# Output projection over heads 0, 1, 2 and 4 as filler of the fourth head's attention and recurrence

## The chip, the cores and the metric

The kernel runs on one core of one Trainium2 chip. The metric is the time of one execution on the device, in microseconds (us). TensorE is called PE in the profile's rows, VectorE DVE, ScalarE ACT, GpSimd POOL; SP is the engine whose queue issues nearly all DMAs.

## The reference, cut to what matters

One encoder layer over 1024 tokens of width 1024, all in float32. Four attention heads and four recurrent heads work side by side on the normalised input; their eight outputs of 128 columns are put next to each other and go through one output projection:

```
h = rmsnorm(x); proj = h @ w_in
o_da = diff_attention(...)       # 4 heads: softmax map 0 - lam * softmax map 1, times v; rmsnorm
o_hg = hgrn2_bidirectional(...)  # 4 heads: gated linear recurrence, both directions; rmsnorm * silu(g)
x = x + concatenate([o_da, o_hg]) @ w_out
x = x + conv_glu(rmsnorm(x), ...)
x = x + (p @ w_ple) * sigmoid(rmsnorm(x) @ w_ple_gate)
out = rmsnorm(x)
```

The change is about the last attention and recurrent heads and the line with `w_out`.

## The kernel before, in words

Every large matrix product is made of three float32r products (high by high, high by low, low by high part), which `mm3` (L151) issues; `split_into` (L143) makes the two parts, the high one on ScalarE, the low one on VectorE or GpSimd.

The program is written as generators. `attn(h)` (L631) yields after each step: a step is the scores of one tile of 128 queries against 1024 keys, with both softmax maps at once in the two buffers B of PSUM (L656), negated maxima on VectorE (L662), exponentials on ScalarE (L664) and their combination on VectorE (L670); or the transposes and value matmuls of the tile before (L682, L686). `hgrn(h)` (L465) yields after each of seven levels (L486 to L509): eight matmuls into a buffer B, updates of K, Y and F on VectorE and GpSimd, and a masked copy of B into A on VectorE (L508). It then yields "v", and goes on with K transposed, the states, the 22 output matmuls (L542 to L546, two matrix passes each), the norm and the transposed output `oT[4 + h]`. The outputs of heads 0, 1, 2, 4, 5, 6 (`SPILLED`, L29; numbers from 4 on are the recurrent heads) are stored to DRAM (`od`, L730), and `head` (L736) loads them again and splits them.

`filler` (L1374) is one stream of the other products: the input projections of the heads, in order, and at the end the first half of the output projection, `out_a`. The stream carries marks ("hq3": head 3's q and gates are done; "hv3": its v and g). `fill(mark)` draws from the stream until the mark comes, or until it is empty; `fill(None, t)` draws until pieces of t us, by the numbers in the yields, are taken, and passes over marks. The loop at the end of `build` (L1423) puts them together for each head: 13 or 14 steps of attention, `fill("hq")`, then the recurrent head, each of its steps followed by one step of attention, and at "v" the rest of the attention and `fill("hv")`.

The order in which these are written is not the order in which they run. When the program is built (`schedule_with_timeline_sim=True`), a planner with its own durations picks, for each engine, among the instructions that are ready and have their buffers, those written first; what is written later moves up where an engine would be idle. `load` (L163) ties a DMA issue to stand behind the last store but one (`lag`) on SP's queue. On the chip each engine runs its list in that fixed order.

`out_a` (L755) multiplies the four attention heads (four `osp` tiles with both parts) by the first 512 rows of `w_out`, 16 pieces (`out_piece`, L748) of 128 tokens by 512 columns, and adds each piece to the rows of x that `load_x` has put into eight buffers of the pool `c` (15 buffers). `out_b` (L790) multiplies the four recurrent heads by the other 512 rows, adds, stores the sum to `xd` in DRAM, and goes on with the norm, the transposes and the first units of the gated MLP.

Of the kernel before, what the change touches and what calls it, by code (L numbers as in the profile page):

```python
# [16 lines left out]
P = 128  # L17
# [5 lines left out]
TAIL = "tail"  # L23
# [3 lines left out]
MAGIC = 12582912.0  # L27

SPILLED = (0, 1, 2, 4, 5, 6)  # L29

_PI_DIGITS = "3.14159265358979323846264338327950288419716939937510582097494459230781640628620899"

# [38 lines left out]
class Net:  # L71
# [155 lines left out]

    def setup(self):
        nc, t, g = self.nc, self.t, self.g
        cst = g.tile([P, 136], F32, name="cst")  # L230
        nc.scalar.dma_start(out=cst, in_=t["cst"])
        self.ident = cst[:, 0:128]
        self.invf = cst[:, 128:136]
        self.gb = self.gb_load("norm_mix_g")

        z = self.small(P, "warm", bufs=1)
        nc.gpsimd.memset(z, 0.0)
        ps = self.Sm()
        for _ in range(18):
            nc.tensor.matmul(ps[:, 0:128], z, z, start=True, stop=True)  # L240

    def setup2(self):
        nc, t, g = self.nc, self.t, self.g
        self.msk = g.tile([P, 8, P], U8, name="msk")
        mf = self.c([8, P])
        nc.sync.dma_start(out=mf, in_=t["msk"])
        nc.gpsimd.tensor_copy(self.msk, mf)
        st = self.c([P])
        nc.gpsimd.memset(st, 0.0)
        nc.sync.dma_start(out=st[0:66, :], in_=t["ffn_conv_w"].rearrange("o j (f p) -> (o j f) p", p=P))  # L250
        nc.sync.dma_start(out=st[66:88, :], in_=t["ffn_conv_b"].rearrange("o (f p) -> (o f) p", p=P))
        nc.sync.dma_start(out=st[88:104, :], in_=t["hg_lb_gamma"].rearrange("z l (h p) -> (z l h) p", p=P))
        nc.sync.dma_start(out=st[104:105, :], in_=t["da_subln_g"])
        nc.sync.dma_start(out=st[105:106, :], in_=t["hg_norm_g"])
        ps = self.Sm()
        nc.tensor.transpose(ps[:, 0:128], st, self.ident)
        cols = self.cols = g.tile([P, P], F32, name="cols")
        nc.vector.tensor_copy(cols, ps[:, 0:128])
        self.cw = lambda j, f: cols[:, j * 22 + f: j * 22 + f + 1]
        self.cb = lambda f: cols[:, 66 + f: 67 + f]  # L260
        self.norm_g = cols[:, 105:106]
        self.subln = g.tile([P, 1], F32, name="subln")
        nc.vector.tensor_scalar(self.subln, cols[:, 104:105], 1.0 - LAMBDA_INIT, None, ALU.mult)

        gam = cols[:, 88:104].rearrange("p (z l h) -> p z l h", z=2, l=2)
        mx = self.small(8, "lbm").rearrange("p (z h) -> p z h", z=2)
        e0 = self.small(8, "lb0").rearrange("p (z h) -> p z h", z=2)
        e1 = self.small(8, "lb1").rearrange("p (z h) -> p z h", z=2)
        nc.vector.tensor_tensor(out=mx, in0=gam[:, :, 0, :], in1=gam[:, :, 1, :], op=ALU.max)
        nc.vector.tensor_tensor(out=e0, in0=gam[:, :, 0, :], in1=mx, op=ALU.subtract)  # L270
        nc.vector.tensor_tensor(out=e1, in0=gam[:, :, 1, :], in1=mx, op=ALU.subtract)
        nc.scalar.activation(e0, e0, AF.Exp)
        nc.scalar.activation(e1, e1, AF.Exp)
        nc.vector.tensor_tensor(out=e1, in0=e0, in1=e1, op=ALU.add)
        nc.vector.reciprocal(e1, e1)
        self.lb = g.tile([P, 2, 4], F32, name="lb")
        self.lb1 = g.tile([P, 2, 4], F32, name="lb1")
        nc.vector.tensor_tensor(out=self.lb, in0=e0, in1=e1, op=ALU.mult)
        nc.vector.tensor_scalar(self.lb1, self.lb, -1.0, 1.0, ALU.mult, ALU.add)

        lam = self.c([4, 64])
        for i, nm in enumerate(("lam_q1", "lam_k1", "lam_q2", "lam_k2")):
            nc.sync.dma_start(out=lam[:, i, :], in_=t[nm].to_broadcast([P, 64]))
        nc.vector.tensor_tensor(out=lam[:, 0, :], in0=lam[:, 0, :], in1=lam[:, 1, :], op=ALU.mult)
        nc.vector.tensor_tensor(out=lam[:, 2, :], in0=lam[:, 2, :], in1=lam[:, 3, :], op=ALU.mult)
        ls = self.small(2, "lam")
        nc.vector.tensor_reduce(ls, vw(lam, [[128, 2], [1, 64]]), AX.X, ALU.add)
        nc.scalar.activation(ls, ls, AF.Exp)
        self.nlam = g.tile([P, 1], F32, name="nlam")
        nc.vector.tensor_tensor(out=self.nlam, in0=ls[:, 1:2], in1=ls[:, 0:1], op=ALU.subtract)  # L290
        nc.vector.tensor_scalar(self.nlam, self.nlam, -LAMBDA_INIT, None, ALU.add)

    def setup_rotary(self):
# [47 lines left out]
        for shift, nm in ((0.25, "cos16"), (0.0, "sin16")):  # L341
            v.tensor_scalar(r, acc, shift, None, ALU.add)
            rnd(q, r)
            v.tensor_tensor(out=r, in0=r, in1=q, op=ALU.subtract)
            v.tensor_scalar(r, r, 6.283185307179586, 3.1415925, ALU.mult, ALU.min)
            v.tensor_scalar(r, r, -3.1415925, None, ALU.max)
            tab = g.tile([P, 8, 2, 8], F32, name=nm)
# [376 lines left out]
        self.spill(h)  # L724


    def wout(self, r0, n, mk=None, lo_eng=None):
        return self.wrows(self.t["w_out"][0], r0, n * 512, 4, mk, lo_eng)

    def spill(self, i):  # L730

# [13 lines left out]
            else:  # L745
                self.split_into(hi, lo, self.oT[i][:, sl.start + o:sl.start + o + 512])

    def out_piece(self, s, n, wp, sp):  # L748
        ps = self.D()
        sl = slice(s * 128, s * 128 + 128)  # L750
        self.mm3(ps, [((sp[k][0][:, sl], sp[k][1][:, sl]), wp[k]) for k in range(4)])
        xs = self.xr[s][:, n * 512:n * 512 + 512]
        self.nc.vector.tensor_tensor(out=xs, in0=ps, in1=xs, op=ALU.add)

    def out_a(self):  # L755

        wp = self.wout(0, 0)
        yield
        sp = []
        for k in range(4):  # L760
            if k == 3:
                yield "heads"
            t = self.d([2, 1024], F32R, name="osp")
            self.head(t, k, slice(0, 1024))
            sp.append((t[:, 0, :], t[:, 1, :]))
        self.load_x()
        yield "x"
        for n in range(2):
            for s in range(NS):
                self.out_piece(s, n, wp, sp)  # L770
                yield 2.6
            if n == 0:
                wp = self.wout(0, 1)

# [15 lines left out]
    def out_b(self):  # L790

        nc = self.nc
        gb = self.gb_load("norm_ffn_g", self.wf([1024]))
        wps = [self.wout(512, 0, lo_eng=nc.vector),
               self.wout(512, 1, lambda: self.w2([2, 512]))]
        sp = None
        self.T = {}
        wg, wu = self.t["w_ffn_gate"][0], self.t["w_ffn_up"][0]
# [3 lines left out]
        for s in range(NS):  # L802
            if s % 4 == 0:
                sl = slice(s * 128, s * 128 + 512)
                sp = []
                for k in range(4):
                    o = self.c([2, 512], F32R, "osp")
                    self.head(o, 4 + k, sl)
                    sp.append(o)
            for n in range(2):  # L810
                ps = self.D()
# [98 lines left out]
        self.t_put("t4", t4, o, p)  # L910

    def load_x(self):
        nc, t = self.nc, self.t
        self.xr = []
        for i in range(8):
            xt = self.c([1024], name="x")
            self.load(out=xt, in_=t["x"][0, i * 128:(i + 1) * 128, :])
            self.xr.append(xt)

    def gb_load(self, name, gb=None):  # L920
# [407 lines left out]
    def build(self):  # L1328
# [4 lines left out]
        with tc.tile_pool(name="xa", bufs=8) as px:  # L1333
# [80 lines left out]
            def fill(mark=None, t=1e9):  # L1414

                while t > 0:
                    c = next(f, mark)
                    if c == mark:
                        return
                    if isinstance(c, float):  # L1420
                        t -= c

            for h in range(4):  # L1423
                at = self.attn(h, qk[h], v[h])
                for _ in range((13, 14, 14, 14)[h]):
                    next(at)
                fill("hq%d" % h)
                hg = self.hgrn(h, st[h])
                for c in hg:
# [4 lines left out]
                    if c is TAIL and h == 3:  # L1434
                        fill("x")
                if h < 3:
                    fill("da%d" % (h + 1))
                    fill(None, (15.6, 10, 10)[h])
                else:
                    fill()  # L1440
# [37 lines left out]
```

## Time and profile before

| | us |
|---|---|
| median of 3 runs | 1577.94 (1577.73 to 1578.14) |
| profiled execution | 1578.55 |
| its span | 1576.7 |
| TensorE busy | 1509.4 (96%) |
| VectorE busy | 1085.8 (69%) |
| GpSimd busy | 699.5 (44%) |
| ScalarE busy | 646.1 (41%) |

The span is the time from the first to the last instruction of the profiled execution; about 1.85 us of that execution lie around it. Busy times are of one execution. The granted clock is given as a share of TensorE's full speed, where the chip has two levels, 1.2 and 2.4 GHz; a value between is a mix of both in the stretch. A value in brackets behind a row of the timeline is the time that the engine was idle before, and the instruction whose end let it go on.

### The profile page before, as it was taken

How to read it: one execution, taken by the hardware profiler on the slowest of the kernel's cores; microseconds unless marked ns; L12 is line 12 of the kernel's file. 1: busy time of each engine (PE TensorE's matmuls, PEld its weight loads, DVE VectorE, ACT ScalarE, POOL GpSimd, SP SyncE). 2: the span in 40 equal slices, each digit the busy share in tenths (PEclk: the TensorE clock that was granted, in tenths of full speed). 3: DMA queues.
4: the chain of work that ended last, by engine and by line, in shares of the span. 5: the costliest groups of instructions: out<-in, count | busy, mean ns of one | idle time of the engine just before them, and what ended most of it. 6: DMA issues, size and time to landing. Idle time of an engine off the chain costs nothing. (4 is left out here: it accounts for less than half of the span.)

```text
span 1576.7 us, 21836 instructions
## 1 busy us (share of the span) xinstructions
PE 1509.4 (96%) x8550; PEld 1298.0 (82%) x8550; DVE 1085.8 (69%) x1617; ACT 646.1 (41%) x1082; POOL 699.5 (44%) x438
## 2 busy tenths in 40 slices
PE   8999999999999997999999999999999899899997
PEld 8969998999799885888778888888887677687886
DVE  7355576555655666757877766666658999986665
ACT  5335525642456255514543333333334233343222
POOL 3111541243105410520577666666657888785000
PEclk9999999999999998999999999999999899999999
DMA  8100011001100111213512222232227632131111
GB/s 247 41 14 15 28 54 41 28 28 41 41 15 28 54 54 40 104 58 130 165 29 93 91 83 87 85 95 82 90 85 251 203 107 80 31 120 47 34 51 40
DMA packets 92201, 118.59 MB, mean 75 GB/s; under 512 B 5200, under 2 KB 65858, under 8 KB 92098
## 3 DMA queue, kind: packets, MB, share of 16 engines
q1 hardware_dynamic: 91666, 116.34, 22.6%
q8 instruction: 67, 1.10, 0.3%
q10 hardware_dynamic: 432, 0.86, 0.2%
q14 instruction: 36, 0.29, 0.1%
HBM read 92.01 MB, written 23.07 MB: 73 GB/s over the span
## 5 line engine op out<-in xcount | busy, mean ns | idle before, releaser
L156 PE MATMUL D<-w,hT 128*128 128x256 f32 x1920 | 256.8, 289 | 0.7 <-POOL w L149 0.3
L156 PEld LDWEIGHTS D<-w,hT 128*128 128x128 f32 x1920 | 239.1, 193 | 3.1 <-issue 1.4
L149 POOL TENSOR_TENSOR w<-raw,w 128x1024 fp32r<-128x1024 f32 x41 | 101.8, 2486 | 277.8 <-ACT w L146 225.0
L156 PE MATMUL E<-T,S 128*128 128x512 f32 x924 | 217.1, 394 | 4.3 <-DVE ag L996 1.7
L149 POOL TENSOR_TENSOR S<-w,S 128x512 fp32r<-128x512 f32 x119 | 171.9, 1459 | 91.8 <-ACT S L146 71.6
L156 PEld LDWEIGHTS E<-T,S 128*128 128x128 f32 x924 | 175.3, 190 | 43.1 <-DVE ag L996 2.1
L156 PE MATMUL D<-hT,w 128*128 128x512 f32 x576 | 138.6, 396 | 0.0
L156 PEld LDWEIGHTS D<-hT,w 128*128 128x128 f32 x576 | 107.2, 189 | 24.7 <-issue 3.2
L156 PE MATMUL S<-T,S 128*128 128x512 f32 x528 | 124.2, 389 | 1.0 <-DVE T L149 1.0
L146 ACT ACTIVATE S<-w 128x512 fp32r<-128x512 f32 x121 | 73.3, 624 | 119.0 <-PE S L156 49.3
L156 PE MATMUL E<-op,op 128*128 128x512 f32 x432 | 107.5, 401 | 10.2 <-DVE x L1118 6.6
L156 PEld LDWEIGHTS S<-T,S 128*128 128x128 f32 x528 | 99.1, 188 | 22.0 <-DVE T L149 1.4
L156 PEld LDWEIGHTS E<-op,op 128*128 128x128 f32 x432 | 82.9, 194 | 31.6 <-DVE x L1118 8.3
L662 DVE TENSOR_REDUCE atm<-B 128x1 f32<-128x1024 f32 x64 | 75.3, 1218 | 44.2 <-PE B L656 44.2
L156 PE MATMUL D<-T,S 128*128 128x512 f32 x396 | 95.1, 391 | 4.1 <-ACT S L146 2.5
L149 POOL TENSOR_TENSOR S<-raw,S 128x512 fp32r<-128x512 f32 x30 | 47.4, 1580 | 99.1 <-ACT S L146 99.1
L156 PE MATMUL D<-w,osp 128*128 128x512 f32 x384 | 90.7, 392 | 0.0
L156 PEld LDWEIGHTS D<-T,S 128*128 128x128 f32 x396 | 73.9, 188 | 20.1 <-ACT S L146 2.7
L664 ACT ACTIVATE e<-B,atm 128x1024 f32<-128x1024 f32 x64 | 70.7, 1112 | 36.4 <-DVE atm L662 36.4
L156 PEld LDWEIGHTS D<-w,osp 128*128 128x128 f32 x384 | 71.2, 188 | 14.4
L156 PE MATMUL B<-wg,h 128*128 128x512 f32 x336 | 80.1, 393 | 0.0
L146 ACT ACTIVATE w<-raw 128x1024 fp32r<-128x1024 f32 x44 | 46.6, 1060 | 79.7 <-PE D L156 62.4
(288 smaller groups left out, 2937.0 us busy)
## 6 DMA issues: line engine op xcount, KB each, us to landing
md<-ag SPq DMA_DIRECT2D x22, 512.0 KB, 2.7
raw<-in_w_in SPq DMA_DIRECT2D x40, 256.0 KB, 3.2
raw<-in_w_ffn_gate SPq DMA_DIRECT2D x20, 512.0 KB, 3.9
w<-in_w_ffn_up SPq DMA_DIRECT2D x20, 512.0 KB, 3.9
mb<-md SPq DMA_DIRECT2D x40, 256.0 KB, 4.7
x<-in_x SPq DMA_DIRECT2D x16, 512.0 KB, 6.8
raw<-in_w_in SPq DMA_DIRECT2D x12, 512.0 KB, 4.0
raw<-in_w_ffn_down SPq DMA_DIRECT2D x12, 512.0 KB, 4.7
```

What stands on the lines that cost most here:

```text
L146: nc.scalar.activation(hi, src, AF.Copy)
L149: (lo_eng or nc.vector).tensor_tensor(out=lo, in0=src, in1=f32(hi), op=ALU.subtract)
L156: m = self.nc.tensor.matmul(out, a, b, start=new and i == 0 and j == 0, stop=i == n - 1 and j == 2, skip_group_check=not new)
L662: nc.vector.tensor_reduce(nm[:, m:m + 1], sc, AX.X, ALU.max, negate=True)
L664: self.last_exp = nc.scalar.activation(em, sc, AF.Exp, bias=nm[:, m:m + 1], accum_out=(s0 if m == 0 else s1)).ins
```

## The change

The first half of the output projection takes heads 0, 1, 2 and 4 (three attention heads and the first recurrent one), the second half heads 3, 5, 6 and 7. `wout` takes a list of heads and loads the weights of each by itself. `out_a` no longer keeps x on the chip: each piece loads its part of x into a buffer of the pool `raw` (3 buffers), adds, and stores the sum to `xd`; `load_x` loads `xd` when all pieces are done. For head 3, attention no longer runs ahead: after "hq3" each step of the recurrent head is followed by two steps of attention, and each but the one at "v" by 4.5 us of filler. The small constants, which had a tile each, become parts of one tile of 800 columns.

```diff
+FIRST, LAST = (0, 1, 2, 4), (3, 5, 6, 7)
...
+        G = g.tile([P, 800], F32, name="cst")
+        cst, self.g_cols, self.g_msk = G[:, 0:136], G[:, 136:264], G[:, 264:520]
+        self.g_rot = [G[:, 520 + 128 * i:648 + 128 * i] for i in range(2)]
...
-    def wout(self, r0, n, mk=None, lo_eng=None):
-        return self.wrows(self.t["w_out"][0], r0, n * 512, 4, mk, lo_eng)
+    def wout(self, heads, n, mk=None, lo_eng=None):
+        w, out = self.t["w_out"][0], []
+        for q in range(0, len(heads), 2):
+            mk = mk or (lambda: self.w([2, 512]))
+            hi, lo = mk(), mk()
+            raw = self.raw([2, 512])
+            for k in range(2):
+                r0 = heads[q + k] * P
+                self.load(out=raw[:, k, :], in_=w[r0:r0 + P, n * 512:n * 512 + 512])
+            self.split_into(hi, lo, raw, lo_eng or self.nc.gpsimd)
+            out += [(hi[:, k, :], lo[:, k, :]) for k in range(2)]
+        return out
...
     def out_a(self):
-        wp = self.wout(0, 0)
+        x = self.t["x"][0]
+        wp = self.wout(FIRST, 0)
         yield
         sp = []
-        for k in range(4):
-            if k == 3:
-                yield "heads"
+        for i in FIRST:
             t = self.d([2, 1024], F32R, name="osp")
-            self.head(t, k, slice(0, 1024))
+            self.head(t, i, slice(0, 1024))
             sp.append((t[:, 0, :], t[:, 1, :]))
-        self.load_x()
-        yield "x"
         for n in range(2):
+            cs = slice(n * 512, n * 512 + 512)
             for s in range(NS):
-                self.out_piece(s, n, wp, sp)
+                ps = self.D()
+                rs, sl = slice(s * P, (s + 1) * P), slice(s * 128, s * 128 + 128)
+                xs = self.raw([512])
+                self.load(out=xs, in_=x[rs, cs])
+                self.mm3(ps, [((sp[k][0][:, sl], sp[k][1][:, sl]), wp[k]) for k in range(4)])
+                self.nc.vector.tensor_tensor(out=xs, in0=ps, in1=xs, op=ALU.add)
+                self.store(out=self.xd[s][:, cs], in_=xs)
                 yield 2.6
             if n == 0:
-                wp = self.wout(0, 1)
+                wp = self.wout(FIRST, 1)
...
-        wps = [self.wout(512, 0, lo_eng=nc.vector),
-               self.wout(512, 1, lambda: self.w2([2, 512]))]
+        wps = [self.wout(LAST, 0, lo_eng=nc.vector),
+               self.wout(LAST, 1, lambda: self.w2([2, 512]))]
...
-                    self.head(o, 4 + k, sl)
+                    self.head(o, LAST[k], sl)
...
-            self.load(out=xt, in_=t["x"][0, i * 128:(i + 1) * 128, :])
+            self.load(out=xt, in_=self.xd[i])
...
-            for h in range(4):
+            for h in range(3):
                 at = self.attn(h, qk[h], v[h])
-                for _ in range((13, 14, 14, 14)[h]):
+                for _ in range((13, 14, 14)[h]):
                     next(at)
                 fill("hq%d" % h)
...
+            fill("hq3")
+            at = self.attn(3, qk[3], v[3])
+            for c in self.hgrn(3, st[3]):
+                next(at, None)
+                next(at, None)
+                if c == "v":
+                    self.run(at)
+                    fill("hv3")
+                elif isinstance(c, float):
+                    fill(None, 4.5)
+            fill()
+            self.load_x()
```

## Rows read from the trace of the kernel before

**Rows 1.** The page's slices: TensorE's busy tenths, and its granted clock.

```profile
PE   8999999999999997999999999999999899899997
PEclk9999999999999998999999999999999899999999
```

**Rows 2.** Windows: stretch, its length, then busy time of each engine, clock, DMA.

```profile
440.00:480.00 40.00, 40.00 (x331) 36.66 (x329) 22.29 (x38) 24.36 (x54) 5.97 (x3) 1.00 0.05 15
...
587.00:641.00 54.00, 40.63 (x280) 34.51 (x281) 34.72 (x56) 31.22 (x74) 7.15 (x5) 0.91 0.15 49
641.00:680.00 39.00, 36.21 (x265) 33.59 (x264) 32.72 (x42) 15.93 (x29) 23.04 (x23) 1.00 0.26 95
...
575.00:723.00 148.00, 130.69 (x866) 115.19 (x865) 97.06 (x163) 66.44 (x126) 37.39 (x30) 0.97 0.20 70
...
590.00:600.00 10.00, 7.47 (x39) 5.97 (x38) 6.37 (x10) 4.63 (x11) 0.00 (x0) 0.67 0.32 105
```

**Rows 3.** Waits of TensorE, 575 to 723: total, times, longest.

```profile
PE B L656 <- ACT e L664: 11.8, 6, 2.6
```

**Rows 4.** Timeline of TensorE, 555 to 740: start, duration, instruction.

```profile
581.30 4.55 PE L156 MATMUL D<-w,hT 128*128 128x256 f32 x36
...
589.48 3.45 PE L686 MATMUL S<-v,wT 128*128 128x128 f32 x16
...
610.95 1.65 PE L656 MATMUL B<-qkT,qkT 64*128 64x512 f32 x12 [2.17 <-ACT e L664]
...
613.02 2.01 PE L686 MATMUL S<-v,wT 128*128 128x128 f32 x16
...
617.64 1.65 PE L656 MATMUL B<-qkT,qkT 64*128 64x512 f32 x12 [2.17 <-ACT e L664]
...
642.28 2.88 PE L156 MATMUL D<-w,hT 128*128 128x256 f32 x22
...
648.72 4.08 PE L156 MATMUL D<-w,hT 128*128 128x256 f32 x32
652.64 1.95 PE L494 MATMUL B<-Y,X 128*128 128x128 f32 x16
...
714.21 22.04 PE L156 MATMUL D<-w,osp 128*128 128x512 f32 x96
```

**Rows 5.** Timeline of ScalarE, the g/v projection's first copy of head 3.

```profile
640.09 0.39 ACT L457 ACTIVATE v<-D 128x256 f32<-128x256 f32 x1
```

**Rows 6.** Timelines of VectorE and of GpSimd near 661.

```profile
661.34 2.89 DVE L504 TENSOR_TENSOR Y<-Y,F 128x512 f32<-128x512 f32 x1
664.15 1.32 DVE L508 COPY_PREDICATED A<-msk,B 128x1024 f32<-128x1024 uint8 x1
...
661.12 2.55 POOL L149 TENSOR_TENSOR w<-raw,w 128x1024 fp32r<-128x1024 f32 x1 [2.76 <-ACT w L146]
```

**Rows 7.** Timelines of TensorE, VectorE and ScalarE at recurrent head 3's end.

```profile
696.66 0.38 PE L546 MATMUL B<-St,Y 128*128 128x128 f32 x2
...
701.12 0.39 PE L544 MATMUL B<-St,Y 128*128 128x128 f32 x2
...
703.50 0.69 DVE L557 TENSOR_TENSOR o<-B,gs 128x512 f32<-128x512 f32 x1 [7.54 <-ACT sq L556]
...
711.97 0.69 DVE L563 TENSOR_TENSOR o<-o,hgy 128x512 f32<-128x512 f32 x1
...
714.06 0.69 ACT L570 ACTIVATE oT<-S,cols 128x512 f32<-128x512 f32 x1 [8.28 <-PE S L569]
```

**Rows 8.** DMA issues: count, size of each, median us to landing.

```profile
raw<-in_w_in SPq DMA_DIRECT2D x40, 256.0 KB, 3.2
...
x<-xd SPq DMA_DIRECT2D x8, 512.0 KB, 5.3
```

**Rows 9.** Timelines of SP's queue and of ScalarE.

```profile
667.44 0.42 SPq L167 DMA_DIRECT2D x<-in_x  x1
...
661.51 1.06 ACT L146 ACTIVATE w<-raw 128x1024 fp32r<-128x1024 f32 x1 [0.46 <-PE D L156]
```

More of the change, by code (lines that the diff above doesn't have):

```diff
@@ L229, in setup @@
         nc, t, g = self.nc, self.t, self.g
-        cst = g.tile([P, 136], F32, name="cst")
+        G = g.tile([P, 800], F32, name="cst")
+        cst, self.g_cols, self.g_msk = G[:, 0:136], G[:, 136:264], G[:, 264:520]
+        self.g_rot = [G[:, 520 + 128 * i:648 + 128 * i] for i in range(2)]
+        self.g_lb = [G[:, 776 + 8 * i:784 + 8 * i] for i in range(2)]
+        self.subln, self.nlam = G[:, 792:793], G[:, 793:794]
         nc.scalar.dma_start(out=cst, in_=t["cst"])
@@ L243, in setup2 @@
         nc, t, g = self.nc, self.t, self.g
-        self.msk = g.tile([P, 8, P], U8, name="msk")
+        self.msk = self.g_msk.bitcast(U8).rearrange("p (l t) -> p l t", l=8)
         mf = self.c([8, P])
@@ L256, in setup2 @@
         nc.tensor.transpose(ps[:, 0:128], st, self.ident)
-        cols = self.cols = g.tile([P, P], F32, name="cols")
+        cols = self.cols = self.g_cols
         nc.vector.tensor_copy(cols, ps[:, 0:128])
@@ L261, in setup2 @@
         self.norm_g = cols[:, 105:106]
-        self.subln = g.tile([P, 1], F32, name="subln")
         nc.vector.tensor_scalar(self.subln, cols[:, 104:105], 1.0 - LAMBDA_INIT, None, ALU.mult)
@@ L275, in setup2 @@
         nc.vector.reciprocal(e1, e1)
-        self.lb = g.tile([P, 2, 4], F32, name="lb")
-        self.lb1 = g.tile([P, 2, 4], F32, name="lb1")
+        self.lb, self.lb1 = [a.rearrange("p (z h) -> p z h", z=2) for a in self.g_lb]
         nc.vector.tensor_tensor(out=self.lb, in0=e0, in1=e1, op=ALU.mult)
@@ L288, in setup2 @@
         nc.scalar.activation(ls, ls, AF.Exp)
-        self.nlam = g.tile([P, 1], F32, name="nlam")
         nc.vector.tensor_tensor(out=self.nlam, in0=ls[:, 1:2], in1=ls[:, 0:1], op=ALU.subtract)
@@ L346, in setup_rotary @@
             v.tensor_scalar(r, r, -3.1415925, None, ALU.max)
-            tab = g.tile([P, 8, 2, 8], F32, name=nm)
+            tab = self.g_rot[len(self.rot)].rearrange("p (t j f) -> p t j f", t=8, j=2)
             rv = r.rearrange("p (t f) -> p t f", t=8)
@@ L746, in head @@
                 self.split_into(hi, lo, self.oT[i][:, sl.start + o:sl.start + o + 512])
[L748 to L753, printed above, removed]
     def out_a(self):
-        wp = self.wout(0, 0)
+        x = self.t["x"][0]
+        wp = self.wout(FIRST, 0)
         yield
         sp = []
-        for k in range(4):
-            if k == 3:
-                yield "heads"
+        for i in FIRST:
             t = self.d([2, 1024], F32R, name="osp")
-            self.head(t, k, slice(0, 1024))
+            self.head(t, i, slice(0, 1024))
             sp.append((t[:, 0, :], t[:, 1, :]))
-        self.load_x()
-        yield "x"
         for n in range(2):
+            cs = slice(n * 512, n * 512 + 512)
             for s in range(NS):
-                self.out_piece(s, n, wp, sp)
+                ps = self.D()
[5 more added lines that the diff above has]
+                self.store(out=self.xd[s][:, cs], in_=xs)
                 yield 2.6
             if n == 0:
-                wp = self.wout(0, 1)
+                wp = self.wout(FIRST, 1)
     def w2(self, shape, dt=F32R):
@@ L912, in load_x @@
     def load_x(self):
-        nc, t = self.nc, self.t
         self.xr = []
@@ L1421, in fill @@
                         t -= c
-            for h in range(4):
+            for h in range(3):
                 at = self.attn(h, qk[h], v[h])
-                for _ in range((13, 14, 14, 14)[h]):
+                for _ in range((13, 14, 14)[h]):
                     next(at)
                 fill("hq%d" % h)
-                hg = self.hgrn(h, st[h])
-                for c in hg:
+                for c in self.hgrn(h, st[h]):
                     next(at, None)
@@ L1433, in build @@
                         fill("hv%d" % h)
[L1434 to L1440, printed above, removed]
+                fill("da%d" % (h + 1))
+                fill(None, (15.6, 10, 10)[h])
+            fill("hq3")
[10 more added lines that the diff above has]
+            self.load_x()
         with tc.tile_pool(name="xb", bufs=4) as pw2, tc.tile_pool(name="xt", bufs=4) as pct:
```

## The prediction

> **What bounds the kernel now.** I first read the 40 slices of the page: TensorE is busy in nearly all of the span, with one dent in mid-kernel, at slice 16, where its granted clock dips too [rows 1]. So TensorE is the bound, and a change can only win what TensorE loses. The windows then size the dent. Between 575 and 723 us TensorE is busy 130.69 of 148 us, so 17.31 us are idle; 13.37 of these lie in 587 to 641 and 2.79 in 641 to 680, which leaves 1.15 for the rest. While attention of an earlier head runs with input projections beside it (440 to 480), nothing is idle [rows 2]. The list of waits names the loss: 11.8 us of score matmuls waiting for the exponentials of the tile before [rows 3]. The timeline shows why nothing fills these waits. The last head's g/v projection stops at 585.85 and goes on at 642.28 [rows 4]; its copies out of PSUM come only at 640.09 [rows 5]. So for 54 us the attention of head 3 runs by itself, and the recurrent head 3 starts after it. A tile of it, with nothing beside it, takes 6.69 us (610.95 to 617.64) and leaves TensorE idle for 2.17 and a bit more [rows 4].
>
> The same stretch loses clock. 590 to 600 was granted 0.67, a mix of the two levels (1.2 and 2.4 GHz), just after the first idle time [rows 2]. The 16 value matmuls of a tile took 3.45 us there against 2.01 later [rows 4]; two such tiles make 2.9 us, and the score matmuls between them, 1.65 us at full clock [rows 4], an estimated 1.4 more: 4.3 us.
>
> The most that can come back is thus 17.3 + 4.3 = 21.6 us.
>
> **The change, part by part.** *Order of the fourth head.* Attention 3 no longer runs 14 steps ahead; each step of the recurrent head is followed by two attention steps and 4.5 us of filler. No matmul is added or removed: the output projection still has two halves of 16 pieces of 12 matmuls, only with heads 0, 1, 2, 4 first. A piece costs 2.755 us (96 matmuls in 22.04 us [rows 4]). Those heads are done before the fourth head starts, so their 16 pieces (44 us) and the g/v projection (two of its pieces left, 12 us at 4.08 us per 32 matmuls) are there as filler. One step of the new stage holds a score tile (6.69 less 2.2 idle: 4.5 us of TensorE), a level of the recurrence (1.95 us) and two pieces (5.5 us), 12 us in all. Its chain without filler is a tile of 6.69, then a level of 1.95 on TensorE, then its masked copy of 1.32 on VectorE [rows 4, 6]: both use the same two PSUM buffers, so they add up, to 10 us. TensorE with filler (12) is longer than the chain (10), so TensorE should set the pace, and the 17.3 us of idle and 4.3 of slow clock go.
>
> What is late next? Four things, each a new idle time.
>
> (a) *The recurrent head's end loses its cover.* In the code, the filler's marks decide this. By the fifth step the g/v projection is used up and its mark has gone by; eight pieces are drawn in steps five to eight, and the call at the recurrence's middle, which looks for that mark, draws all that is left. So the last eight pieces come ahead of the recurrence's second part, and nothing is left beside its end. From the last piece on the chain is: the 44 output matmuls, 696.66 to 701.51, 4.85 us; the square of one half, some 0.6; VectorE's norm, 703.50 to 712.66, 9.2 us with 3.3 us of other work and waiting in it, so 5.9; transposes and the copy with the norm gain, 0.6 + 0.69; the split of head 7 into high and low parts, two operations of that size, 1.4; and some 0.7 in hand-overs: 14.7 us [rows 7]. TensorE's own part is 4.85 + 1.0, and the second half's first two pieces can run over heads 3, 5 and 6 (18 matmuls, 4.1 us) before they need head 7. Idle: 14.7 - 10 = 4.7. Bounds: 0 (the planner strews this chain between the last pieces) and 8.8 (no piece can start early).
>
> (b) *Weights between the two column halves.* The old loads could be issued far ahead. The new ones go behind the store of the seventh piece on SP, since a load is queued behind the last store but one. Landing 3.2 us [rows 8], high part 1.06 [rows 9], low part of two pairs on POOL 2.55 each [rows 6]: 9.4 us, plus 1 us for the add and the store's issue, less the eighth piece (2.755) and the parts of two pieces that need only the first pair (2.755): 4.9 us without pieces. The last attention tile and the recurrence's transposes fall here. Bounds 0 and 4.9; I take 2.
>
> (c) *Misses side by side.* The nearest rows are 440 to 480 (none idle) and 641 to 680, levels with pieces (2.79 of 39, 7%) [rows 2]. Over eight steps of 12 us that is 0 to 6.9; I take 4, as half of the chain is of either kind.
>
> (d) *Clock.* Bounds 0 and the 4.3 lost now; the tail's idle share (4.7 of 14.7) is like that of the stretch where the clock fell (13.4 of 54), so some of it returns: 2.
>
> *x by way of DRAM.* Sixteen loads of x by half rows, sixteen stores, and later eight loads of the sums; two issues instead of one for each weight pair (8 more), one more whole spilled head and two fewer half ones: 39 more issues in all, at 0.42 us each 16 us of SP's time over more than 100 us [rows 9]. In each piece three input buffers are in turn: the load goes behind the store of the piece before last, so 0.4 + 0.4 + 3.2 + 0.7 us for the add per two pieces, 4.7 against 5.5 on TensorE [rows 4, 8, 9]. It is hidden, with little to spare: were the landing 1 us longer, each pair of pieces would wait 0.2. The reloads (5.3 us [rows 8]) start with the ninth store, some 19 us before the last piece: hidden by seven pieces; without that cover the first of them costs its 5.3 us. VectorE has the same 16 additions. Behind a store that waits for its addition stand all later loads of SP, the second half's weights among them; this is (b).
>
> *Constants in one tile, second half over heads 3, 5, 6, 7:* 0, as the operations stay; the spilled heads 5 and 6 load under the last pieces. If the constants' single tile made readers wait for later writers, it would show before 120 us; I put 0 to 2 on it and take 0.
>
> Sum: 21.6 won, 4.7 + 2 + 4 + 2 = 12.7 given back: 8.9 us faster. The profiled execution took 1578.55 (span 1576.7 and 1.85 around it); 1578.55 - 8.9 = 1569.65. The median of the runs, 1577.94, lies 0.6 below the profiled one, so I forecast 1569.0.
>
> **A rule against it.** POOL's 2.55 us subtraction at 661.12 and VectorE's product at 661.34 overlapped, and the product took 2.89 us, where one of its shape takes 0.69 [rows 6, 7]. The Trainium skill ("SBUF — State Buffer", section "Who interferes with whom") says that a VectorE instruction with two SBUF inputs and a GpSimd instruction that reads SBUF exclude each other for the whole instruction; the trace agrees. POOL has only 7.15 us of work in the 54 us of attention alone [rows 2]; side by side, attention's combination of two maps runs into the levels' POOL work for the first time. By the rule each such meeting holds the chain up by as much as 2.2 us, which is the first rival.
>
> **Rivals.** *1, slower: the chain sets the pace.* The queues are fixed at build time, so where a step's chain is late, the pieces queued behind its matmul are late too. It decides from 12 us per step: each step then costs 8 times the excess. With one VectorE meeting of 2.2 us and a second wait for the PSUM pair of 2 us, 10 becomes 14.2, and 8 x 2.2 = 17.6 us more: 1569 + 17.6 = 1586.6. For it: the reserve is only 2 us; TensorE waited for exactly such a product, as VectorE's slow row at 661 shows. Against: VectorE is busy for 34.7 and 32.7 us in the two stretches that are laid over each other, 67 us in 97 [rows 2].
> *2, no change: the end without cover.* (a) at 8.8, (b) at 4.9, (d) at 4.3, (c) at 4: 22 given back, 1578. For it: nothing is left as filler. Against: three heads' part of the first two pieces does not need the tail.
> *3, better: the planner strews the tail.* (a) 0, (b) 1, (c) 3, (d) 0.5: 17 won, 1561. For it: in 641 to 723 it laid pieces between the recurrence's steps.
> *4, the change does not do what it says:* the first half's weights or heads come too late, and the fourth attention still runs alone: 1575 to 1579, a part of rival 2.
>
> **How the numbers follow.** A difference of 0.2% (3.2 us) can be told from no change. Forecast (1564 to 1574.8) 0.45; rival 3 (1556 to 1564) 0.18; rivals 2 and 4 (1574.8 to 1581) 0.18; rival 1 (above 1581) 0.19. Faster 0.63, same 0.18, slower 0.19. The range, 1559 to 1584, leaves out some 0.1 at each end; the forecast's own is 1564 to 1575.
>
> **What would show it.** Right: value and score matmuls of head 3 with output-projection and g/v pieces between them from about 580 on; no window of 40 us with over 3 us idle before the end of the first half; an idle time of about 5 us just ahead of the second half, with the norm's VectorE steps as its chain; at most 5 us without pieces between the column halves. Wrong: score or level matmuls waiting 2 us or more in each step, with VectorE named (rival 1); a TensorE gap over 8 us before the second half (rival 2); sum loads landing after the second half's first addition, or a difference before 540 us, where the work is unchanged.

## The result, and the profile after

The changed kernel takes 1597.70 us (median of 4 runs, 1596.27 to 1599.84) against 1577.84 for the kernel before on the same chip (1576.06 to 1578.14): a ratio of 1.0129, 95% interval 1.0117 to 1.0142. It is 20 us slower; I had forecast 9 faster. The prediction was wrong in its sign.

The profiled execution has a span of 1596.0 us, 19.3 more than before. At 558 us the two traces are within 0.1 us of each other, so the constants' tile and the earlier heads cost nothing. The page's slices of the kernel after, TensorE's busy tenths and granted clock:

```profile
PE   8999999999999999967989999999999899899997
...
PEclk9999999999999999978999999999999999999999
```

Against [rows 1] the dent has moved from slice 16 to slices 18 and 19 and has become deeper. Windows of the kernel after (stretch, length, TensorE busy, clock, DMA share, GB/s) size it:

```profile
575.00:600.00 25.00, 25.00 (x198) 1.00 0.19 65
600.00:674.00 74.00, 71.88 (x397) 1.00 0.38 125
674.00:707.50 33.50, 20.66 (x122) 0.76 0.37 125
707.50:737.50 30.00, 19.88 (x144) 0.84 0.21 74
```

The idle time that I wanted gone is gone: up to 674 only 2.1 of 99 us are idle. After it 12.8 and 10.1 us are idle, at clocks between the two levels (0.76 and 0.84). Over the whole stretch, 575 to 737.5, TensorE is idle for 25.1 us (17.3 before [rows 2]) and busy for 137.4 (130.7 before) with the same matmuls. The second half of the projection starts at 737.48; before, it started at about 722.5 (its first 60 matmuls end with the 96 at 736.25 [rows 4]). It is 15.0 later: 7.8 are idle time, and 7.2 are more busy time at the slower clock (0.5 us of the 130.7 fall into 722.5 to 723 and belong to the second half). Of the other 4.3 of the 19.3 us, 2.4 follow at once: the first 60 matmuls of the second half take 16.32 us (granted 0.88 in 737.5 to 760), where a kernel that arrives at full clock takes 13.88 (experiment 12). Some 2 us are strewn over the rest.

TensorE's waits in 575 to 738, after (total, times, longest):

```profile
PE B L498 <- ACT X L495: 14.0, 4, 7.2
PE S L573 <- DVE o L567: 6.0, 1, 6.0
PE B L550 <- DVE St L540: 2.5, 1, 2.5
PE D L158 <- ACT osp L148: 1.3, 1, 1.3
...
PE D L158 <- DVE raw L781: 0.3, 1, 0.3
```

The first line replaces the one of [rows 3]: it is no longer the scores that wait for exponentials, but the levels' matmuls (L498) that wait for their copies X. The timeline of TensorE after shows where (start, duration; in brackets the idle time before):

```profile
598.98 1.55 PE L158 MATMUL D<-w,osp 128*128 128x512 f32 x6
600.84 0.59 PE L498 MATMUL B<-Y,X 128*128 128x128 f32 x2 [0.32 <-ACT X L495]
...
667.59 6.62 PE L158 MATMUL D<-w,osp 128*128 128x512 f32 x28
674.04 0.38 PE L498 MATMUL B<-Y,X 128*128 128x128 f32 x2
674.79 1.83 PE L498 MATMUL B<-Y,X 128*128 128x128 f32 x14
688.91 0.79 PE L498 MATMUL B<-Y,X 128*128 128x128 f32 x2 [7.17 <-ACT X L495]
690.36 3.35 PE L498 MATMUL B<-Y,X 128*128 128x128 f32 x14
703.74 3.78 PE L498 MATMUL B<-Y,X 128*128 128x128 f32 x16 [5.00 <-ACT X L495]
734.22 1.97 PE L573 MATMUL S<-cst,o 128*128 128x128 f32 x8 [5.98 <-DVE o L567]
737.48 16.32 PE L158 MATMUL D<-w,osp 128*128 128x512 f32 x60 [1.30 <-ACT osp L148]
```

From the first level (600.84) to the fifth (674.04) four steps take 73.2 us, 18.3 each. All 192 matmuls of the 16 pieces lie between 598.98 and 674.2, three to four and a half pieces to a step. Then the filler is spent, with two levels and the whole end of head 3 still to come. A bare step takes 14.8 us (688.91 to 703.74). The same 14 level matmuls cost 1.83 us at 674.79 and 3.35 at 690.36, after 7.17 us of idle time: 1.2 in place of 2.4 GHz.

What fills a bare step is seen on VectorE and ScalarE of the kernel after, from their timelines:

```profile
693.75 0.69 DVE L506 TENSOR_TENSOR Y<-Y,F 128x512 f32<-128x512 f32 x1 [2.64 <-PE B L498]
694.36 0.68 DVE L508 TENSOR_TENSOR Y<-Y,F 128x512 f32<-128x512 f32 x1
694.97 1.30 DVE L512 COPY_PREDICATED A<-cst,B 128x1024 f32<-128x1024 uint8 x1
697.96 2.36 DVE L666 TENSOR_REDUCE atm<-B 128x1 f32<-128x1024 f32 x2 [1.70 <-PE B L660]
...
700.35 1.11 ACT L668 ACTIVATE e<-B,atm 128x1024 f32<-128x1024 f32 x1 [3.50 <-DVE atm L666]
...
701.46 1.10 ACT L668 ACTIVATE e<-B,atm 128x1024 f32<-128x1024 f32 x1
...
702.55 1.14 ACT L495 ACTIVATE X<-K 128x512 f32<-128x512 f32 x2
```

A level must leave its PSUM buffer (L512) before the score tile may use both; the tile's two exponentials must be through before the next level may have one. And ScalarE, idle before 700.35, makes the next X only behind both exponentials. It is one closed ring: level, masked copy, scores, maxima, exponentials, X, level.

### The profile page after: what moved, and what is told of

Read it like the earlier page. It is cut to its first block, busy times and chain, and to the rows that moved or that the text cites. A ratio compares the mean times of both kernels' runs of the same rounds, so it can differ in the third digit from the quotient of the medians.

```text
span 1596.0 us, 21901 instructions
## 1 busy us (share of the span) xinstructions
PE 1516.6 (95%) x8550; PEld 1302.1 (82%) x8550; DVE 1089.7 (68%) x1617; ACT 643.1 (40%) x1081; POOL 714.1 (45%) x438
## 5 line engine op out<-in xcount | busy, mean ns | idle before, releaser
L151 POOL TENSOR_TENSOR S<-w,S 128x512 fp32r<-128x512 f32 x119 | 179.5, 1524 | 89.3 <-ACT S L148 68.7
L158 PE MATMUL D<-w,osp 128*128 128x512 f32 x384 | 94.1, 401 | 1.6 <-ACT osp L148 1.3
L498 PE MATMUL B<-Y,X 128*128 128x128 f32 x448 | 64.4, 298 | 16.3 <-ACT X L495 14.0
```

The source lines that it names most:

```text
L151: (lo_eng or nc.vector).tensor_tensor(out=lo, in0=src, in1=f32(hi), op=ALU.subtract)
L158: m = self.nc.tensor.matmul(out, a, b, start=new and i == 0 and j == 0, stop=i == n - 1 and j == 2, skip_group_check=not new)
L498: nc.tensor.matmul(ps[:, c * 128:(c + 1) * 128], X[:, c * 128:(c + 1) * 128], vw(Y, [[2 * hh, 64 // hh], [1024 + hh, 2], [1, hh]], c * 128 ...
```

## The experiments

In the first four expectations, theory A is the ring: its chain sets the pace, uses up the filler early and leaves the end bare. In experiments 3 and 4 it comes in two kinds, by X's buffer in SBUF and by the PSUM pair. Rival R is the route: x by way of DRAM, with 39 more DMA issues and the three input buffers. All ratios are to the kernel before, with 95% intervals.

**1. The old order of the fourth head put back, the rest of the change kept.**

```diff
-            fill("hq3")
             at = self.attn(3, qk[3], v[3])
+            for _ in range(14):
+                next(at)
+            fill("hq3")
             for c in self.hgrn(3, st[3]):
                 next(at, None)
-                next(at, None)
...
-                elif isinstance(c, float):
-                    fill(None, 4.5)
```

> Only the order of the fourth head goes back: attention 3 runs 14 steps ahead, the recurrent head has one attention step per step, and the filler is drawn at the marks. Heads 0, 1, 2, 4 first, x by way of DRAM and the one constants tile stay. Theory A (pace: a score tile and a recurrence level that take turns at the two PSUM buffers make a chain of 15 us a step, which uses up the filler early and leaves the end bare): the loss goes, 1574 to 1582, score tiles at 6.7 us again. Rival R (the route: 39 more DMA issues, sums to DRAM and back, three raw buffers): the loss stays, 1590 or more.

1597.77 us, 1.0129 [1.0106, 1.0153]: the loss stays, as rival R had it, and theory A misses. Its waits of TensorE, 575 to 760:

```profile
PE D L158 <- ACT osp L148: 14.8, 2, 13.1
PE B L660 <- ACT e L668: 13.4, 6, 4.7
```

The ring is gone, the old dent is back (second line, against [rows 3]), and a new wait stands just ahead of the second half: `D` for `osp`, 14.8 us in two waits. So what is left of the change, the route of x or the choice of heads, has a price of its own, which the side-by-side order hides. Experiment 5 tells which.

**2. The new order of the fourth head alone, in the kernel before.**

```diff
-            for h in range(4):
+            for h in range(3):
...
+            fill("hq3")
+            at = self.attn(3, qk[3], v[3])
+            for c in self.hgrn(3, st[3]):
+                next(at, None)
+                next(at, None)
...
```

> The other half of the change alone: the kernel before, its output projection over heads 0 to 3 with x kept on the chip, but the fourth recurrent head and attention side by side, two attention steps per step. There is no filler beside the steps here. Theory A: seven steps of 12.5 to 15 us each, 88 to 104 us, against 54 + 38 us one after the other, and then the pieces: 1590 to 1605. Rival R: no change, 1574 to 1582.

1617.51 us, 1.0258 [1.0227, 1.0288]: 40 us slower, theory A's way and beyond its range. Heads 0 to 3 still come first, so no piece is ready before attention 3 ends, and the ring runs bare. One window of it (columns as above):

```profile
575.00:700.00 125.00, 82.43 (x495) 0.78 0.04 14
```

Some 43 us idle; TensorE waits 36.5 us in seven waits for X. The order alone is the worst version of all.

**3. X of head 3 from pool c in place of the temporaries' pool.**

```diff
-            X = self.c2([1024], name="X")
+            X = (self.c if h == 3 else self.c2)([1024], name="X")
```

> The changed kernel, with the level's operand X of head 3 taken from pool c instead of pool c2, which it shares with the exponentials. Buffers of a pool are handed out in written order, so in the changed kernel X of a level comes behind the two exponentials. If that is what makes the step long (A, buffers in SBUF): a bare step falls from 14.8 to 12.5 us or less, and the time to 1585 to 1593. If the two PSUM buffers make it (A, PSUM), or under R: 1594 to 1600, the bare step stays within 1 us.

1588.92 us, 1.0076 [1.0052, 1.0099]: some 9 us back, in the range of theory A by X's buffer. Its timeline of TensorE:

```profile
684.16 3.78 PE L498 MATMUL B<-Y,X 128*128 128x128 f32 x16 [4.70 <-ACT e L668]
...
697.16 2.05 PE L498 MATMUL B<-Y,X 128*128 128x128 f32 x16 [2.90 <-ACT e L668]
...
729.17 15.87 PE L158 MATMUL D<-w,osp 128*128 128x512 f32 x60 [1.30 <-ACT osp L148]
```

The levels now wait for the exponentials (the PSUM buffer), no longer for X; the bare step is 13.0 us (12.5 or less was expected), and the second half starts 8.3 earlier. So X had waited for a buffer of the pool that it shares with the exponentials' tiles, not for its data.

**4. The levels of head 3 in the two other PSUM buffers (D).**

```diff
-            ps = self.B()
+            pd = [self.D(), self.D()] if h == 3 else None
+            ps = None if h == 3 else self.B()
...
```

> The changed kernel, with the levels of head 3 in two PSUM buffers of D (half each, so two masked copies) instead of one of B; the pieces of the projections share D with them. A, PSUM: tile and level no longer take turns, the step is 8 to 11 us, the filler lasts to the recurrence's end, 1565 to 1580. A, buffers in SBUF: step above 13 us, 1590 or more, as X stays where it was. R: 1595 to 1600.

1597.30 us, 1.0131 [1.0111, 1.0151]. The time is in rival R's range and not in theory A's, yet the trace changed. Levels of it:

```profile
608.82 1.13 PE L500 MATMUL D<-Y,X 128*128 128x128 f32 x8
...
670.96 1.06 PE L500 MATMUL D<-Y,X 128*128 128x128 f32 x8
...
672.63 1.06 PE L500 MATMUL D<-Y,X 128*128 128x128 f32 x8
...
728.17 1.94 PE L580 MATMUL S<-cst,o 128*128 128x128 f32 x8 [12.92 <-DVE hgy L189]
```

The period falls to 12.4 us (608.82 to 670.96 is five steps), and the last level ends at 673.7 in place of 707.5. No level waits for X or for the exponentials any more. But 12.4 and 18.3 us are not the ring's length with and without the shared pair: in 600 to 674 TensorE is busy for 71.7 of 74 us here and 71.9 in the changed kernel, so both are TensorE's own work. What differs is the filler between two levels, two pieces or as much of the g/v projection here. No step of this run is bare, so how much shorter the chain itself became is not shown. And now the pieces come last. The recurrence's 44 output matmuls lie between them, from 692.98 to 714.86 (4.85 us in all before [rows 7]); the second half's weights land only then and are split amid the norm; TensorE waits 12.9 us for it.

**5. The kernel before with x by way of DRAM, nothing else.**

```diff
-        self.load_x()
         yield "x"
...
+                xs = self.raw([512])
+                self.load(out=xs, in_=x[rs, cs])
...
+                self.store(out=self.xd[s][:, cs], in_=xs)
...
-            self.load(out=xt, in_=t["x"][0, i * 128:(i + 1) * 128, :])
+            self.load(out=xt, in_=self.xd[i])
...
```

> The kernel before with one thing changed: each piece of the first half loads its part of x into the three input buffers and stores its sum to DRAM, and the sums are loaded again for the second half; heads 0 to 3 still come first and the fourth head keeps its old order. The run with the old order of the fourth head (1597.8) was no faster than the changed kernel, and its trace shows why: after the last piece TensorE waits 13.1 and 1.7 us for the second half's heads, and 720 to 760 has 22.8 us of work at a clock of 0.74 (39.3 at 1.0 before). Theory H (handover): the pieces' x now turns over in the same three input buffers and on the same queue as the second half's weights and heads, so these can only be loaded when the last pieces are done. Then this kernel is slower too, 1587 to 1600, with 10 us or more of TensorE waits between the halves. Theory F (the choice of heads: the fourth attention head is now needed last): the route is harmless, 1574 to 1581.

1602.12 us, 1.0156 [1.0140, 1.0172]: theory H, and a little over its range. The route alone costs 24 us where the pieces come last. Timelines of TensorE and of SP's queue in it:

```profile
708.64 11.13 PE L156 MATMUL D<-w,osp 128*128 128x512 f32 x48
739.46 16.07 PE L156 MATMUL D<-w,osp 128*128 128x512 f32 x60 [19.69 <-ACT osp L146]
...
718.18 0.38 SPq L167 DMA_DIRECT2D raw<-in_w_out  x1
...
727.09 0.38 SPq L167 DMA_DIRECT2D raw<-in_w_out  x1
...
733.31 8.99 SPq L167 DMA_DIRECT2D raw<-od  x6
```

The second half's weights and spilled heads need the three input buffers that the pieces' x now turns over. They are issued from 718 to 742. In the kernel before, two of the four loads of these weights go 50 us earlier, the other two at 697, and the heads from 711.96. SP's queue before:

```profile
663.70 3.65 SPq L167 DMA_DIRECT2D raw<-in_w_out  x2
...
697.25 0.89 SPq L167 DMA_DIRECT2D raw<-in_w_out  x2
```

**6. Experiment 1 with the pieces' x in tiles of pool d** (which the input's transposes leave free).

```diff
-                xs = self.raw([512])
+                xs = self.d([2, 1024])[:, 0, 0:512]
```

> The first experiment's kernel (heads 0, 1, 2, 4 first, old order of the fourth head), with the pieces' x in tiles of the pool d, which is free by then, in place of the three input buffers. Theory H: the second half's weights and heads get the input buffers early again; the hole at 720 to 760 goes, most of 20 us: 1576 to 1584. Theory Q (the hole is made by the queue's order, stores and reloads ahead of the weights, not by the buffers): 1590 to 1600.

1589.45 us, 1.0068 [1.0046, 1.0091]. Between the two: 8 of the 20 us come back, and one wait of 11.1 us is left of two that made 14.8. The buffers are part of the handover's price. Timelines of SP's queue, ScalarE and TensorE show what ends the wait that is left:

```profile
721.61 0.81 SPq L169 DMA_DIRECT2D raw<-in_w_out  x2
...
727.91 1.06 ACT L148 ACTIVATE w<-raw 128x1024 fp32r<-128x1024 f32 x1 [8.89 <-DMA raw<-in_w_out]
...
729.54 2.07 PE L158 MATMUL D<-w,osp 128*128 128x512 f32 x4 [11.12 <-ACT osp L148]
```

ScalarE splits the heads only behind the last pair of weights, whose loads still go as late as 721.61. Whether an input buffer or the order on SP's queue holds these loads there, no run separates.

**7. The changed kernel with its second eight pieces held behind the last level**, x in pool d as in 6.

```diff
-                self.mm3(ps, ...)
+                with self.after(self.level if n else None):
+                    self.mm3(ps, ...)
...
```

`self.after(m)` lets what stands in it be issued only behind the instruction m, here the last matmul of the last level.

> The changed kernel with the pieces of its second column half held behind the last level of the recurrence, and the pieces' x in tiles of pool d (so that the second half's weights are not shut out of the input buffers). In the changed kernel all 16 pieces are used up by 674, and 674 to 738 has 23 us of idle TensorE at a clock of 0.80. Theory U (cover used up too early): the eight held pieces fill most of the recurrence's end, the clock stays up there, and about 10 us come back: 1583 to 1590. Theory C (the chain of score tile and level sets the pace, its period 14.8 us bare against 17.7 covered): the steps that lose their cover get only 3 us shorter each and stand idle in turn, the hole moves from the end into the levels: 1590 to 1600, with more idle in 575 to 674 than the 2.1 us of the changed kernel.

1603.53 us, 1.0168 [1.0153, 1.0183]: worse than the change, as theory C had it, and by more. The windows of it:

```profile
640.00:696.00 56.00, 33.87 (x187) 0.73 0.00 1
696.00:738.00 42.00, 37.80 (x219) 0.95 0.63 219
738.00:755.00 17.00, 9.73 (x39) 0.70 0.39 141
```

The hole moves into the levels. Two of them:

```profile
635.12 0.49 PE L498 MATMUL B<-Y,X 128*128 128x128 f32 x2 [1.47 <-ACT X L495]
...
647.85 0.79 PE L498 MATMUL B<-Y,X 128*128 128x128 f32 x2 [5.59 <-ACT X L495]
```

The first bare step, whose matmuls still run at full clock, takes 12.7 us; the next three take 15 each, at the slow clock. The held pieces then stretch the recurrence's end, whose matmuls queue behind them, and the norm is bare all the same (second half at 748.97). So to hold half of the cover back moves the hole and does not close it. That the cover is used up too early is not ruled out by this: the eight free pieces went four and a half and three to a step, as in the changed kernel, into the first two steps. No run lets them go two by two in this order.

**8. Experiment 4 with the pieces' x in pool d.** The edit is that of 6 on top of 4.

> The changed kernel with the levels of head 3 in their own two PSUM buffers (in the fourth run these cut the period of a step from 17.7 to 12.4 us, and the last level came 31 us earlier, yet the time stayed at 1597: the pieces then took turns at 3.4 us each behind their x, and TensorE stood still for 17 us before the second half) and with the pieces' x in tiles of pool d. Theory H (what kept that gain was the handover by the shared input buffers): 1578 to 1588. Theory E (it was the recurrence's own end, its output matmuls queued behind pieces and its norm bare): 1590 to 1598.

1584.55 us, 1.0048 [1.0034, 1.0062]: 13 us back over experiment 4, within theory H's range. The norm's wait falls from 12.9 to 6.2 us, and the second half starts at 725.05. So the shared PSUM pair and the handover together account for most of the 20 us; the changed kernel with x in pool d and nothing else was not run. The fourth head side by side is still 7 us behind the kernel before.

**9. The kernel before, attention head 3's output tile from the temporaries' pool.**

```diff
-        oT = self.oT[h] = (self.c2 if h in SPILLED else self.c)([1024], name="oT")
+        oT = self.oT[h] = (self.c2 if h in SPILLED or h == 3 else self.c)([1024], name="oT")
```

> The kernel before with one buffer moved: the output tile of attention head 3 comes from the pool of the attention's temporaries in place of the pool c. Theory B (buffers are handed out in written order, and the fourth head's v and gate tiles stood behind this tile, which is first written at 639.5): the g/v projection, 12 us, then runs between the score tiles of attention 3, TensorE's idle time in 587 to 641 falls from 13.4 to under 6 us; the recurrence then has less cover, so the time gains less: 1566 to 1575. Theory A0 (attention 3 alone has another reason, such as readiness of the weights): no change, 1574 to 1579.

1570.28 us, 0.9953 [0.9938, 0.9969]: faster than before by one buffer. Its window, against the second row of [rows 2] (40.63 at 0.91):

```profile
587.00:641.00 54.00, 48.17 (x359) 41.97 (x358) 33.16 (x52) 35.73 (x75) 12.15 (x6) 0.97 0.34 118
```

5.8 us idle in place of 13.4. This is what made attention 3 run alone: the copies of v and the gate had no buffer of pool c. Whether the pool was one short, or handed its buffers out in the written order (these copies are written behind that tile's first use, and ran 0.6 us after it, 639.52 and 640.09), one run does not tell. The dent that the change was to fill was for its larger part a matter of one tile's pool.

**10. The first ideas together**: experiment 6, the output tile of 9, and the pieces let go one by one along the chain.

```diff
+                with self.after(self.mark[(None, None, None, None, 'l0', 'l1', 'l2', 'l3', 'l4', 'l5', 'l6', 'l6', 'k0', 'k1', 'po', 'po')[n * 8 + s]]):
...
```

> Heads 0, 1, 2, 4 first and the old order of the fourth head, with three things: the pieces' x in tiles of pool d, attention 3's output tile from the pool of temporaries, and the 16 pieces let go one by one: four at once, six behind the first six levels, two behind the last level, two behind the two state products, two behind the output matmuls of the recurrence. If the three causes found so far (handover, buffer order, cover used up too early) are all of it, the stretch 575 to 723 loses most of its 17 idle us: 1560 to 1568. If a covered chain is stretched by its own cover as much as it hides (each piece holds a ready matmul up), there is no gain: 1574 to 1582.

1580.38 us, 1.0012 [1.0002, 1.0022]: no gain, a miss for the first theory. Attention 3 is covered (50.15 of 54 us busy in 587 to 641), but 5.0 us are idle in 641 to 680 and 8.1 in 680 to 721.

**11. The change's choice of heads, x kept on the chip**, old order, head 3 spilled like the others, pieces let go one by one.

```diff
-SPILLED = (0, 1, 2, 4, 5, 6)
+SPILLED = (0, 1, 2, 3, 4, 5, 6)
+FIRST, LAST = (0, 1, 2, 4), (3, 5, 6, 7)
...
```

> The change's choice of heads without its route and without its side by side: heads 0, 1, 2, 4 first, head 3 stored and loaded again like them, x kept on the chip as before, old order of the fourth head; the pieces are let go one by one (three at once, five behind levels, two behind the last, one and two behind the state products, three behind the output matmuls). If the choice of heads is good in itself and the route by DRAM is what spoils it, pieces run in attention 3's waits and nothing is lost at the handover: 1562 to 1569. If the second half suffers from a head that is ready late and has to come from DRAM: 1572 to 1582.

1575.22 us, 0.9988 [0.9978, 0.9997]. In the range of the second forecast and as good as no change: the choice of heads is harmless, and no gain without the rest.

**12. Experiment 9 with the last pieces held for the recurrence's end.**

```diff
+        with self.after(self.mark[(None, None, None, None, None, None, None, 'l6', 'l6', 'k0', 'k1', 'k1', 'po', 'po', 'po', 'po')[n * 8 + s]]):
...
```

> The kernel before with attention head 3's output tile in the pool of temporaries (1570.3 against 1578.2), and its pieces held so that more of them cover the recurrence's end: seven as before, two behind the last level, one behind the first state product, two behind the second, four behind the output matmuls (there were two). In the run without the holds TensorE waited 3.9 us for the norm and the clock was 0.91 in 680 to 720. If the cover at the end is worth its idle and its clock: 1564 to 1568.5. If the levels lose as much as the end gains: 1569 to 1573.

1566.45 us, 0.9930 [0.9914, 0.9946]: 11 us faster than the kernel before and 31 faster than the change. Its window and the start of its second half:

```profile
680.00:715.00 35.00, 34.08 (x185) 29.12 (x184) 21.56 (x58) 9.90 (x14) 4.74 (x2) 1.00 0.19 66
...
708.73 13.88 PE L156 MATMUL D<-w,osp 128*128 128x512 f32 x60 [0.92 <-ACT osp L146]
```

The clock stays at full speed to the end, the second half starts 13.8 us earlier than before.

## Why the prediction was wrong

**The bound was read rightly.** 17.3 us of idle time and 4.3 of slow clock were there to be won; experiment 12 wins 11.

**The step that failed is the one on the new stage: "TensorE with filler (12) is longer than the chain (10), so TensorE should set the pace".** It did as long as there was filler: up to 674 only 2.1 us are idle. But a step got three to four and a half pieces and not the two of my sum, took 18.3 us and not 12, and the 16 pieces were gone after four steps. My count of filler per step came from the program's text (4.5 us by step); the planner moves pieces up wherever it sees a gap. From there on the chain set the pace, and the chain is 14.8 us, not 10. My sum of it was 6.69 + 1.95 + 1.32. It lacked the two updates of Y that stand ahead of the masked copy on VectorE (0.69 + 0.68: 693.75 to 696.27 in place of 1.32), the copies X, which come behind both exponentials (1.14; experiment 3 shows that they need not), and the clock: the level and one score matmul take 4.8 us (688.91 to 693.71) where 674.04 to 676.62 is 2.6. That is 1.2 + 1.1 + 2.2, which with hand-overs gives the 4.8 that is missing. At full clock the chain is 12.7 us (experiment 7). With 6.5 us of its own work on TensorE (4.5 + 1.95) such a step has room for two pieces, so the number in my sum would about have filled it; the order that was built gave it up to twice as many at first and none at the end.

**Rival 1 was the mechanism, in part.** It said that the chain sets the pace, at 14.2 us per step, and gave 1586.6. The length was near the bare step's 14.8, in part by luck, as 2.2 of these are the clock, which it did not name; the place and the price were not right. I had the loss in pieces queued late behind a slow chain; it came as a bare chain once the pieces were spent, and bare time costs clock as well. Of its two reasons the PSUM pair is borne out in part: on buffers of their own no level waits for X or the exponentials (experiment 4), though how much of the chain that saves is not shown. The other, VectorE held up by GpSimd, is small: the product at L506 took 1.79 and 2.68 us in the first and third level in place of 0.69, 3.1 us in all, under cover. (The two stretches that it lays over each other are 93 us long, not 97; nothing hangs on it.)

**(a) The end without cover** was priced at 4.7 idle (0 to 8.8). 10.1 us are idle in 707.5 to 737.5: 6.0 on the norm, 2.5 on the states, which the term did not have, 1.3 on the split of head 7 and small ones. The mechanism was right, the term too small (7.6 without the states): the first pieces of the second half did not start early.

**(b) Weights between the column halves** were priced at 2: no wait for them in 575 to 738; 0. **(c) Misses side by side**, 4: 2.1 in 575 to 674. Both were too high, and it did not matter.

**(d) The clock**, 2: 7.2 us more busy time for the same matmuls up to 737.5, and 2.4 in the 60 behind it, 9.6 in all. I let the clock follow idle time as in the old dent, and the idle time itself was wrong.

**x by way of DRAM** was called hidden, and in the changed kernel it is: 0.3 us of waits for `raw`, and the second half's weights go out from 672.67, long before they are needed. But the reason that I gave (queue time) was not the one that matters. It is hidden because the pieces are done 63 us early. Experiment 5 shows its price where they are not: 24 us. So the change's parts do not add up: the order alone costs 40, the route alone 24, both together, with heads 0, 1, 2 and 4 first, 20, since early pieces pay for the ring's bare time and hide the route.

**The reason for the old dent** I had only half: I saw that the g/v projection stops at 585.85 and its copies come at 640.09 [rows 4, 5], and took attention's place in the program for the cause. It was the copies' buffer, which experiment 9 frees.

What stays open: why side by side with both repairs (experiment 8) is still 7 us slower, though 575 to 600, with 9.5 idle us at a clock of 0.80, is the largest piece of it; whether the ring would have lasted with two pieces to a step; the 2 us that the change loses behind the start of its second half, and which of the two reasons in experiment 9 holds.

## What to carry to other kernels

Before a latency chain is put beside another, write the ring that they form through shared buffers, every operation between two uses of the same buffer, on every engine, and divide the cover by its number of turns; a buffer that both use makes the lengths add up. Then look at how the order that is built deals the cover out: more than the gap of a turn makes that turn longer and leaves a later one bare. Where work stands idle that has its data, look first for the buffer that it waits for, and whose first use is written ahead of it; moving one tile to another pool can do what a reordering was meant to do. Price each part of a change alone and with the others: here both costly parts hid each other.

## What the runs showed of the hardware

GpSimd holds up VectorE even for tiny operations. In experiment 4, timelines of GpSimd and VectorE:

```profile
721.38 4.64 POOL L151 TENSOR_TENSOR w<-raw,w 128x1024 fp32r<-128x1024 f32 x2 [28.02 <-ACT w L148]
...
721.45 2.30 DVE L180 TENSOR_SCALAR hgy<-hgq 128x4 int32<-128x4 int32 x1
723.66 0.15 DVE L188 TENSOR_TENSOR hga<-hga,hgq 128x4 f32<-128x4 f32 x1
723.78 2.25 DVE L187 TENSOR_TENSOR hga<-hgy 128x4 f32<-128x4 f32 x1
```

Two operations on four elements per partition took 2.30 and 2.25 us, each until one of GpSimd's two subtractions ended; operations of this size take 0.15 to 0.17 when nothing runs there. The split of the second half's weights thus put 4.2 us into the norm that the second half waits for. The Trainium skill ("SBUF — State Buffer", section "Who interferes with whom") says that the engine that issues first holds the ports that the two share for its whole instruction, and the other is blocked, not slowed; these rows agree.

The clock charges idle time twice. In the kernel after, the stretch with 23 us of idle time ran on at 0.76 and 0.84, and the first 60 matmuls behind it still took 16.32 us. In experiment 12, with no such hole ahead, 60 of the same shape took 13.88 at a granted clock of 1.00.
